# A two-layer hybrid decoder trunk: x taken in transposed, keys' blocks moved ahead of the values' blocks, one matmul per head for compressed values

## The chip, the cores and the metric

One Trainium2 chip, one core of it. The metric is the device time of one launch in microseconds, lower is better. Inputs and outputs lie in the chip's memory; arrays that the kernel prepares on the host before the launch (constants, and after the change a transposed copy of x) are not in the time.

## What is computed

x is 512 tokens by 1024 channels, float32. Two layers, each a token mixer and a feed-forward block, with RMS norms ahead of both:

```python
h = rms_norm(x, norm_mix_g[i]);  proj = h @ w_in[i]        # q_r k_r v_r g_r q_n kv_n gates
y_ret = (silu(g_r) * groupnorm(retention(rot(q_r), rot(k_r), v_r))) @ w_o_ret[i]
kc = gelu((blocks(k_c) + pos_k) @ w1_k) @ w2_k             # 31 blocks of 32 tokens, stride 16
vc = gelu((blocks(v_c) + pos_v) @ w1_v) @ w2_v
o_n = g0 * softmax(q kc + bias) vc + g1 * selected(q, k_s, v_s) + g2 * softmax(q k_w + bias) v_w
x = x + (sigmoid(m_a) * y_ret + sigmoid(m_b) * (o_n @ w_o_nsa[i])) @ w_out[i]
x = x + (silu(a) * b) @ w_ffn_out[i]                        # a, b from rms_norm(x) @ w_ffn_in[i]
```

NSA (the second mixer) has 16 heads of width 64 in two groups, with compressed keys and values of their own.

## The kernel before

Activations lie with channels on the partitions, x as 8 tiles of 128 channels by 512 tokens. A float32 product is made of three passes: each operand is split in a high part (a rounded copy, ScalarE) and the rest (VectorE), and `mm3` (L118 to L124) multiplies high by high, low by high and high by low. The norm's factor per token is not put into the activations: `make_h` splits x times the gain, and the factor 1/rms, kept as a row on all partitions in `rb`, is multiplied in where a product leaves PSUM. So a projection can start before the statistics are done, but what is read from its bank waits for `rb`.

A weight block comes as 1 MB into one of 3 raw buffers (`raw`, L91, on SP's queue) and is split by `cut` into pieces of 128x1024: the high part `wh` on ScalarE (L79), the low part `wl` on VectorE (L80). There are 3 buffers for pieces (`WH = 3`), so a fourth piece waits until TensorE has done with the first.

Start (`setup`, `start_x`): x is loaded as it lies, tokens on partitions, in 8 tiles; TensorE transposes it (L259, 32 transposes), ScalarE copies (L262) and splits it (L83), VectorE makes the low part (L84) and the sums of squares (L256). The gains and position embeddings are loaded as rows in 7 small DMAs and transposed as well (L158). GpSimd's queue writes the transposed x to memory (L266) for the residual.

`nsa_kv` is the stage that the change turns over, once per layer. On TensorE: `psc`, two products of 24 matmuls of 512 columns (compressed keys and values before compression); the statistics, `norm_stats` and `norm_bcast`, which makes `rb`; `psk`, two more (keys of the selected and the window branch); `compress` for keys and for values, 32 matmuls of 256 columns each (L377), whose inputs VectorE builds (`z` L352, `xa` L363, `p` or `pt` L80) and whose weight is four pieces (c0 to c3); `q0`, the first two query products of 24 each; then 96 matmuls of 304 columns for values and gates. `compress` and `q0` are generators and the calls of `next` in `nsa_kv` set their order in the code. A scheduler of the framework then sets each engine's final order from the dependences and its own estimates, so that pieces of neighbours may be interleaved.

After it the 16 heads run, with scores, softmax and products merged with gate projections that fill TensorE. Per head `nsa_finish` (L588) adds the compressed branch with two matmuls of 512 columns, one for the high part of the probabilities and one for the low part; `vc` holds a head's 31 rows at the partitions of its place in a quad and zeros elsewhere.

## Time and profile before

| | |
|---|---|
| median of 3 runs | 2456.5 us (2456.14 to 2457.05) |
| the profiled execution: its time, its span | 2455.72 us, 2453.9 us |
| TensorE busy, share of the span | 2404.7 us, 98% |
| VectorE, ScalarE, GpSimd busy | 57%, 42%, 10% |
| chain that ended last: TensorE, VectorE, ScalarE | 89%, 6%, 3% |
| layer 0: first matmul of the first product | at 17.28 us |
| layer 0: first matmul of values and gates | at 73.68 us |
| layer 1: first matmul of its first product | at 1231.50 us |
| layer 1: first matmul of values and gates | at 1285.61 us |

Matmuls overlap, so the recorded length of one (about 0.39 us for 512 columns) is longer than the time it takes from the next; the distance of two starts in a row tells that. Times in views are microseconds from the span's start. In the timeline's rows the columns are start, length (of all that the row merges), engine, line, operation, out<-in, shape, count, and in brackets the idle time ahead of it with what ended it.

### The profile page before, as it was taken

Reading aid. Unit: us, or ns where it says so; the run is one execution under the profiler, and the core shown is the slowest. Engines: PE = TensorE matmul, PEld = TensorE weight load, DVE = VectorE, ACT = ScalarE, POOL = GpSimd, SP = SyncE. Lnnn points to the kernel's source line nnn. Section 1 sums busy time; section 2 is a strip of 40 time slices with the busy share of each in tenths; the row PEclk is TensorE's granted clock in tenths of the full one; section 3 lists DMA queues with packets and bytes.
Section 4 is the critical chain, followed back from the end, with each engine's and each line's share of the span. In section 5 each row is a group of like instructions: output and inputs, shape, how many; then the busy total and the mean of one; then the engine's idle time right before and its main releaser. Section 6 shows DMA issues by size and latency. Waiting matters only on the chain.

```text
span 2453.9 us, 29372 instructions
## 1 busy us (share of the span) xinstructions
PE 2404.7 (98%) x11115; PEld 1956.1 (80%) x11115; DVE 1409.4 (57%) x2797; ACT 1025.3 (42%) x1862; POOL 252.2 (10%) x225
## 2 busy tenths in 40 slices
PE   7999999999999999999989999999999999999998
PEld 5877777888888878888878787778888877888887
DVE  6778886454574633333567878864545654434334
ACT  4666675233333432222346676642333333222222
POOL 1000000010020110110110000001100202101010
PEclk9999999999999999999999999999999999999999
DMA  7523224522342432323454322235223434223221
GB/s 230 149 74 87 74 69 102 165 85 96 98 142 95 155 102 87 103 87 99 128 141 120 94 79 73 74 102 156 90 93 106 159 110 139 86 86 103 86 95 60
DMA packets 234874, 262.47 MB, mean 107 GB/s; under 512 B 42276, under 2 KB 178637, under 8 KB 234733
## 3 DMA queue, kind: packets, MB, share of 16 engines
q1 hardware_dynamic: 220720, 236.93, 32.0%
q10 hardware_dynamic: 13244, 21.41, 2.4%
q8 instruction: 87, 1.43, 0.2%
q0 software_dynamic: 768, 2.27, 0.2%
q14 instruction: 55, 0.44, 0.1%
HBM read 235.36 MB, written 25.21 MB: 106 GB/s over the span
## 4 chain that ended last, share of the span: by engine, by line
PE 89%; DVE 6%; ACT 3%; issue 1%; POOL 1%; DMA 0%; SPq 0%; POOLq 0%; ACTq 0%; DVEq 0%
PE f L123 12%; PE f L122 12%; PE f L124 12%; PE a L124 8%; PE a L123 7%; PE a L122 7%; PE o L124 7%; PE o L122 7%; PE o L123 7%; PE t L573 2%; DVE p L553 1%; PE o L566 1%; PE o L565 1%; PE a L541 1%; PE a L542 1%
## 5 line engine op out<-in xcount | busy, mean ns | idle before, releaser
L79 ACT ACTIVATE wh<-wr 128x1024 fp32r<-128x1024 f32 (+3 forms) x406 | 397.2, 980 | 986.2 <-PE f L123 263.6
L80 DVE TENSOR_TENSOR wl<-wr,wh 128x1024 fp32r<-128x1024 f32 (+3 forms) x406 | 462.7, 1143 | 220.7 <-ACT wh L79 211.9
L122 PE MATMUL f<-hh,wh 128*128 128x512 f32 x936 | 373.4, 400 | 0.7 <-ACT wh L79 0.5
L124 PE MATMUL f<-hh,wl 128*128 128x512 f32 x936 | 371.5, 397 | 1.8 <-DVE wl L80 1.7
L123 PE MATMUL f<-hl,wh 128*128 128x512 f32 x936 | 370.7, 396 | 0.1
L124 PEld LDWEIGHTS f<-hh,wl 128*128 128x128 f32 x936 | 176.7, 189 | 44.0 <-DVE wl L80 4.1
L122 PEld LDWEIGHTS f<-hh,wh 128*128 128x128 f32 x936 | 176.9, 189 | 36.4 <-ACT wh L79 1.4
L123 PEld LDWEIGHTS f<-hl,wh 128*128 128x128 f32 x936 | 176.8, 189 | 33.9 <-DVE hl L84 0.6
L523 ACT ACTIVATE p<-p,nmx 128x512 f32<-128x512 f32 (+3 forms) x256 | 142.3, 556 | 67.1 <-DVE nmx L522 65.0
L80 DVE TENSOR_TENSOR pt<-t,pt 128x512 fp32r<-128x512 f32 (+3 forms) x256 | 123.5, 485 | 56.2 <-ACT pt L79 54.6
L124 PE MATMUL a<-hh,wl 128*128 128x512 f32 x360 | 144.7, 402 | 9.3 <-DVE wl L80 9.3
L122 PE MATMUL a<-hh,wh 128*128 128x512 f32 x360 | 144.8, 402 | 0.0
L123 PE MATMUL a<-hl,wh 128*128 128x512 f32 x360 | 144.5, 401 | 0.0
L79 ACT ACTIVATE pt<-t 128x512 fp32r<-128x512 f32 (+3 forms) x256 | 109.3, 429 | 71.8 <-PE t L573 66.9
L876 POOL TENSOR_TENSOR fa<-fa,rb 128x512 f32<-128x512 f32 x44 | 77.2, 1755 | 570.1 <-ACT fa L875 570.1
L522 DVE CUSTOM_DVE_ANT_0 p<-a,strip 128x512 f32<-128x512 f32 (+3 forms) x256 | 119.5, 484 | 18.1 <-PE a L542 11.5
L122 PE MATMUL o<-hh,wh 128*128 128x512 f32 x304 | 120.1, 395 | 0.0
L124 PE MATMUL o<-hh,wl 128*128 128x512 f32 x304 | 120.0, 395 | 0.0
L123 PE MATMUL o<-hl,wh 128*128 128x512 f32 x304 | 119.9, 395 | 0.0
L573 PE MATMUL t<-ident,p 128*128 128x128 f32 x640 | 113.7, 273 | 0.0
L573 PEld LDWEIGHTS t<-ident,p 128*128 128x128 f32 x640 | 81.3, 141 | 24.3 <-issue 2.2
L565 PE MATMUL o<-pt,vs 128*128 128x512 f32 (+3 forms) x256 | 91.4, 360 | 1.4 <-ACT pt L79 1.4
(423 smaller groups left out, 4859.4 us busy)
## 6 DMA issues: line engine op xcount, KB each, us to landing
wr<-in_w_in SPq DMA_DIRECT2D x66, 1024.0 KB, 5.3
wr<-in_w_ffn_in SPq DMA_DIRECT2D x44, 1024.0 KB, 5.2
wr<-in_w_ffn_out SPq DMA_DIRECT2D x18, 1024.0 KB, 5.0
wr<-in_w_o_ret SPq DMA_DIRECT2D x16, 1024.0 KB, 5.0
wr<-in_w_in SPq DMA_DIRECT2D x36, 256.0 KB, 4.0
strip<-bv SPq DMA_DIRECT2D x32, 256.0 KB, 5.1
gs<-mt ACTq DMA_DIRECT2D x32, 256.0 KB, 2.0
wr<-in_w_o_nsa SPq DMA_DIRECT2D x16, 512.0 KB, 7.3
```

Of the source, the lines that this page charges most:

```text
L79: self.nc.scalar.activation(hi, src, AF.Copy)
L80: (eng or self.nc.vector).tensor_sub(lo, src, hi.bitcast(F32))
L122: self.nc.tensor.matmul(ps, lh, rh, start=start and i == 0, stop=False)
L123: self.nc.tensor.matmul(ps, lh, rl, start=False, stop=False)
L124: self.nc.tensor.matmul(ps, ll, rh, start=False, stop=stop and i == n - 1)
L522: nc.vector.tensor_tensor_reduce(p, src, self.backwards(strip, w - 1, w), -1.0, BIG, ALU.add, ALU.min, nmx[:, c])
L523: nc.scalar.activation(p, p, AF.Exp, scale=-1.0, bias=nmx[:, c], accum_out=sm[:, c])
L541: nc.tensor.matmul(ps[:, :w], qh[:, ts], ks[:, br, :w], start=True, stop=False)
L542: nc.tensor.matmul(ps[:, :w], ql[:, ts], ks[:, br, :w], start=False, stop=True)
L565: nc.tensor.matmul(po[:, j * P :], lhs, th, start=br == 0 and j == 0, stop=False)
L573: nc.tensor.transpose(pt[:, (i - j) * P : (i - j + 1) * P], pr[br][i][:, j * P : (j + 1) * P], self.ident)
L876: nc.gpsimd.tensor_mul(t, t, self.rb)
```

## The change

Four things. (1) The host hands over x transposed (`c_xt`) and the gains and embeddings as columns (`c_cols`). The order on SP's queue becomes: the columns, two tiles of x, the first 1 MB block of weights, six tiles of x, the keys' block, the first queries' block, and then the compression weights. The 33 transposes, the copies, the small loads and the write of x to memory are gone. The sums of squares are now made as in the later norms: squares on ScalarE, seven additions on GpSimd (`acc_sq`), four matmuls with a column of ones. (2) In `nsa_kv`, in both layers, both pieces of the keys' block are cut at once and both products `psk` stand ahead of `compress`; the statistics' second half (`norm_bcast`) stands between them; `compress` of keys runs in one go behind the first query product, that of values behind the second. (3) `norm_bcast` transposes instead of multiplying by the identity. (4) High and low part of the compressed probabilities of two heads share a tile, rows 0 to 63 and 64 to 127, so `nsa_finish` needs one matmul; the splits in `nsa_cmp` become four operations on 64 partitions from two on 128, those in `compress` four pairs from eight.

```diff
@@ setup
-        rows = self.u("rows", w=P)
...
-        self.xnat = []
-        for hf in range(2):
-            for t in range(NT):
-                xt = self.u("xnat")
-                nc.sync.dma_start(xt, a["x"][0, t * P : (t + 1) * P, hf * 512 : (hf + 1) * 512])
-                self.xnat.append(xt)
-            if hf == 0:
-                load_rows()
-        self.setup_bias()
-        ps = self.tp()
-        nc.tensor.transpose(ps[:, :104], rows[:104, :], self.ident[:104, :104])
         self.cols = self.const("cols", [P, 104])
-        nc.vector.tensor_copy(self.cols, ps[:, :104])
+        nc.sync.dma_start(self.cols, a["c_cols"])
...
+        self.setup_bias()
@@ norm_bcast
         for t in range(NT):
-            nc.tensor.matmul(ps[:, t * P : (t + 1) * P], rep[:, t * P : (t + 1) * P], self.ident, start=True, stop=True)
+            nc.tensor.transpose(ps[:, t * P : (t + 1) * P], rep[:, t * P : (t + 1) * P], self.ident)
         nc.scalar.activation(self.rb, ps, AF.Copy)
@@ start_x
-        for k in range(KD):
-            if k % 4 == 0:
-                for t in range(NT):
-                    junk = self.u("junk")
-                    xn = self.xnat[k + t]
-                    nc.vector.tensor_tensor_reduce(junk, xn, xn, 1.0, 0.0, ALU.mult, ALU.add, ss[:, k + t : k + t + 1])
-            ps = self.mm() if k % 2 else self.tp()
-            for t in range(NT):
-                nc.tensor.transpose(ps[:, t * P : (t + 1) * P], self.xnat[4 * (k // 4) + t][:, (k % 4) * P : (k % 4 + 1) * P],
-                                    self.ident)
-            xt = self.u("xt")
-            nc.scalar.activation(xt, ps, AF.Copy)
-            h.append(self.make_h(xt, self.gmix[0][:, k : k + 1]))
-            if k == 2:
-                self.first_h = self.last_hi
-            nc.gpsimd.dma_start(self.xs[k], xt)
+        xts = [self.u("xt") for _ in range(KD)]
+        w = self.a["w_in"][0][:, C_KV : C_KV + 256].rearrange("(k p) n -> p k n", p=P)
+        for k in range(2):
+            last = nc.sync.dma_start(xts[k], self.a["c_xt"][k])
+        with self.tc.issue_after(last.ins):
+            raw = self.raw([(lambda v: v, w)], KD, 256)
+        with self.tc.issue_after(self.last_load.ins):
+            for k in range(2, KD):
+                self.last_x = nc.sync.dma_start(xts[k], self.a["c_xt"][k])
+        h = [self.make_h(xts[k], self.gmix[0][:, k : k + 1]) for k in range(2)]
+        with self.tc.issue_after(self.last_hi.ins):
+            self.first_w = [self.cut(raw[:, :, j * P : (j + 1) * P]) for j in range(2)]
+        h += [self.make_h(xts[k], self.gmix[0][:, k : k + 1]) for k in range(2, KD)]
+        self.first_h = self.last_hi
 
         def stats():
-            s2 = self.small("s2", NT)
-            nc.vector.tensor_add(s2, ss[:, :NT], ss[:, NT:])
-            self.norm_stats(ss=s2)
-            self.norm_bcast()
-
-        self.stats = stats
+            self.bias_rows()
+            acc = None
+            for xt in xts:
+                acc = self.acc_sq(acc, xt)
+            self.norm_stats(acc)
+
+        self.stats = stats, self.norm_bcast
@@ nsa_kv
-        self.stats()
+        self.stats[0]()
...
-        psk = [self.proj_t([self.cut(wk[:, :, :P])], 0, h, "a")]
+        with self.tc.issue_after(self.first_h.ins) if l == 0 else nullcontext():
+            wk = [self.cut(wk[:, :, br * P : (br + 1) * P]) for br in range(2)]
+        psk = [self.proj_t(wk, 0, h, "a")]
+        self.stats[1]()
+        psk.append(self.proj_t(wk, 1, h, "a"))
         comp = {kind: self.compress(l, kind, psc[i]) for i, kind in enumerate("kv")}
-        for kind in "kvk":
-            next(comp[kind])
-        psk.append(self.proj_t([self.cut(wk[:, :, P:])], 0, h, "a"))
+        fill = lambda n: [next(q0, None) for _ in range(n)]
+        next(comp["k"])
+        fill(9)
+        next(comp["k"])
+        next(comp["k"])
+        next(comp["v"])
         keys(0)
-        next(comp["k"])
-        for _ in range(2):
-            for _ in range(9):
-                next(q0, None)
-            next(comp["v"])
+        fill(9)
+        next(comp["v"])
+        next(comp["v"])
         keys(1)
@@ compress
-                    nc.scalar.activation(vc[r, q, :64], src, AF.Copy)
-                    nc.vector.tensor_sub(vc[r, q, 64:], src, vc[r, q, :64].bitcast(F32))
-                self.vc.append(vc)
+            for q in range(4):
+                r = slice(32 * q, 32 * q + 32)
+                nc.scalar.activation(vc[r, :, q % 2, :64], src[r], AF.Copy)
+                nc.vector.tensor_sub(vc[r, :, q % 2, 64:], src[r], vc[r, :, q % 2, :64].bitcast(F32))
+            self.vc = vc
@@ nsa_cmp
-        pc += [self.u("pch", F32R), self.u("pcl", F32R)]
-        self.split(pc[0], pc[1], pt2)
+
+        for r, o in ((slice(0, 64), slice(64, P)), (slice(64, P), slice(0, 64))):
+            x = self.u("pc", F32R)
+            self.split(x[r], x[o], pt2[r])
+            pc.append(x)
@@ nsa_finish
-        for i, x in enumerate(st["pc"]):
-            nc.tensor.matmul(po, self.vc[b][:, s], x, start=False, stop=i == 1)
+        nc.tensor.matmul(po, self.vc[:, b, s % 2], st["pc"][s // 2], start=False, stop=True)
@@ mix
-                nc.vector.tensor_add(xt, ps, self.ld("xo", self.xs[n]))
+                nc.vector.tensor_add(xt, ps, self.ld("xo", self.xs[n] if l else self.a["c_xt"][n]))
```

TensorE in layer 1, the kernel before, where the keys' second product (`a_10356`, pieces `wh_10352`, `wl_10353`) begins within compression of keys (`o_10325`, L377):

```order
L122 MATMUL a_10356<-hh_9912,wh_10352 128x512
L123 MATMUL a_10356<-hl_9913,wh_10352 128x512
L377 MATMUL o_10325<-wh_10391,p_10280 128x256
L124 MATMUL a_10356<-hh_9912,wl_10353 128x512
L122 MATMUL a_10356<-hh_9940,wh_10352 128x512
```

The keys' second product stands here in the middle of the keys' compression, and waits at its third row for `wl_10353`. The same place of the change: compression of keys (`o_10284`, now L362) at its third and fourth piece, behind it the second query product (`f_10393`):

```order
L362 MATMUL o_10284<-wl_10292,p_10219 128x256
L362 MATMUL o_10284<-wh_10313,p_10226 128x256
L362 MATMUL o_10284<-wl_10314,p_10226 128x256
...
L362 MATMUL o_10284<-wh_10317,p_10233 128x256
L362 MATMUL o_10284<-wl_10318,p_10233 128x256
...
L122 MATMUL f_10393<-hh_9829,wh_10389 128x512
L123 MATMUL f_10393<-hl_9830,wh_10389 128x512
L124 MATMUL f_10393<-hh_9829,wl_10390 128x512
```

The keys' products have moved ahead, all four pieces of a compression now follow each other, and the next product needs the fifth piece in a row.

VectorE in layer 0 of the change, from the low part of the last tile of x (`hl_154`) to the first use of `rb`; `wl_253`, `wl_257` are the keys' pieces, `wl_360` the queries', `wl_406` the first piece of compression, `var` and `rep` belong to the statistics:

```order
L84 SCALAR_TENSOR_TENSOR hl_154<-xt_106,cols,hh_153 128x512
L178 COPY near_212<-t_210 16x256
L179 COPY far_213<-t_210 16x384
L80 TENSOR_TENSOR wl_253<-wr_207,wh_252 128x1024
L80 TENSOR_TENSOR wl_257<-wr_207,wh_256 128x1024
L80 TENSOR_TENSOR wl_360<-wr_354,wh_359 128x1024
L80 TENSOR_TENSOR wl_406<-wr_403,wh_405 128x1024
L219 TENSOR_SCALAR var_246<-t_241 128x4
L269 TENSOR_SCALAR hrstd<-rstd 128x4
L225 COPY rep_285<-rstd 128x512
L337 TENSOR_TENSOR z_321<-f_157,rb 64x256 x4
```

Before, `var` stood ahead of three of the cuts of x and of every cut behind the keys' first piece; now it stands behind four cuts.

VectorE in layer 1 of the change, between the two compressions: the inputs of the values' compression (`pt`), the keys' split (`ks`), the second query product's end (`qd`), and the second to fourth piece of the values' compression (`wl_10440`, `wl_10462`, `wl_10466`):

```order
L80 TENSOR_TENSOR pt_10378<-xa_10374,pt_10378 128x4x64
L80 TENSOR_TENSOR ks_10132<-kd_10381,ks_10132 64x512
L80 TENSOR_TENSOR ks_10133<-kd_10381,kh_10382 64x512
L425 SCALAR_TENSOR_TENSOR qd_10418<-f_10393,rb 128x512
L80 TENSOR_TENSOR wl_10440<-wr_10433,wh_10439 128x1024
L80 TENSOR_TENSOR ql_10421<-qd_10418,qh_10420 64x512
L80 TENSOR_TENSOR wl_10462<-wr_10459,wh_10461 128x1024
L80 TENSOR_TENSOR ql_10427<-qd_10418,qh_10426 64x512
L80 TENSOR_TENSOR wl_10466<-wr_10459,wh_10465 128x1024
L80 TENSOR_TENSOR wl_10515<-wr_10511,wh_10514 128x912
```

Three of that compression's four pieces have moved behind the second query product's end, and the values' first piece (`wl_10515`) follows them at once.

## Rows read from the trace of the kernel before

**Rows 1.** The page: busy time (share of the span) and instructions of each engine, and the shares of the chain that ended last.

```profile
PE 2404.7 (98%) x11115; PEld 1956.1 (80%) x11115; DVE 1409.4 (57%) x2797; ACT 1025.3 (42%) x1862; POOL 252.2 (10%) x225
...
PE 89%; DVE 6%; ACT 3%; issue 1%; POOL 1%; DMA 0%; SPq 0%; POOLq 0%; ACTq 0%; DVEq 0%
```

**Rows 2.** The timeline of TensorE in layer 0, from the end of `psc` to the second keys' product.

```profile
35.09 0.39 PE L124 MATMUL f<-hh,wl 128*128 128x512 f32 x1
35.32 0.39 PE L124 MATMUL a<-hh,wl 128*128 128x512 f32 x1
...
44.04 0.28 PE L377 MATMUL o<-wh,p 128*128 128x256 f32 x1
49.17 0.79 PE L124 MATMUL a<-hh,wl 128*128 128x512 f32 x1 [4.86 <-DVE wl L80]
49.77 0.63 PE L122 MATMUL a<-hh,wh 128*128 128x512 f32 x1
...
53.18 0.63 PE L124 MATMUL a<-hh,wl 128*128 128x512 f32 x1
```

**Rows 3.** The windows view: stretch, its length, then busy time (instructions) of PE, PEld, DVE, ACT, POOL, the granted clock, the DMA engines' share, GB/s.

```profile
10.00:12.00 2.00, 0.93 (x4) 0.36 (x2) 0.00 (x0) 1.94 (x4) 0.00 (x0) 1.00 0.91 303
...
50.00:55.00 5.00, 5.00 (x15) 3.85 (x15) 4.23 (x5) 1.89 (x3) 0.00 (x0) 0.60 0.68 210
```

**Rows 4.** The timeline of layer 0's start, all engines: transposes, the first weight block, the low parts, the statistics' power.

```profile
6.61 0.47 PE L259 MATMUL o<-ident,xnat 128*128 128x128 f32 x1
...
16.17 1.06 ACT L79 ACTIVATE wh<-wr 128x1024 fp32r<-128x1024 f32 x1 [2.63 <-DMA wr<-in_w_in]
...
17.34 2.06 DVE L84 SCALAR_TENSOR_TENSOR hl<-xt,cols,hh 128x512 fp32r<-128x512 f32 x3
...
20.60 0.80 PE L124 MATMUL f<-hh,wl 128*128 128x512 f32 x1 [1.67 <-DVE wl L80]
...
26.95 1.48 POOL L235 TENSOR_TENSOR rstd<-var,mhalf 128x4 f32<-128x4 f32 x1 [4.18 <-DVE var L234]
```

**Rows 5.** The timeline of TensorE in layer 1: the wait for the statistics, the wait for the keys' second piece, values and gates.

```profile
1247.37 1.13 PE L244 MATMUL t<-ident,rep 128*128 128x128 f32 x8 [2.72 <-DVE hrstd L289]
...
1261.74 0.50 PE L124 MATMUL a<-hh,wl 128*128 128x512 f32 x1 [4.45 <-DVE wl L80]
...
1285.61 0.30 PE L122 MATMUL a<-wh,hh 128*128 128x304 f32 x1
...
1287.73 0.30 PE L124 MATMUL o<-wh,hl 128*128 128x304 f32 x1
```

**Rows 6.** The timeline of ScalarE in layer 0: `rb`.

```profile
36.88 0.60 ACT L245 ACTIVATE rb<-t 128x512 f32<-128x512 f32 x1 [0.53 <-PE t L244]
```

**Rows 7.** The timeline of VectorE in layer 0: the first piece of the values' block.

```profile
72.73 1.11 DVE L80 TENSOR_TENSOR wl<-wr,wh 128x912 fp32r<-128x912 f32 x1
```

**Rows 8.** The timeline of VectorE in layer 1, from the statistics to the first piece of the values' block.

```profile
1244.94 2.27 DVE L240 COPY rep<-rstd 128x512 f32<-128x512 f32 x1 [1.14 <-POOL rstd L235]
...
1249.16 1.75 DVE L352 TENSOR_TENSOR z<-f,rb 64x256 f32<-64x256 f32 x4 [0.75 <-ACT rb L245]
...
1256.84 2.37 DVE L363 TENSOR_TENSOR xa<-z,cols 128x124 f32<-128x124 f32 x8
1259.13 1.42 DVE L80 TENSOR_TENSOR pt<-xa,pt 128x256 fp32r<-128x256 f32 x4
...
1263.57 0.69 DVE L80 TENSOR_TENSOR ks<-kd,ks 64x512 fp32r<-64x512 f32 x1
...
1271.92 0.42 DVE L384 TENSOR_TENSOR gx<-o,gy 64x256 f32<-64x256 f32 x1
...
1276.32 0.69 DVE L441 SCALAR_TENSOR_TENSOR qd<-f,rb 128x512 f32<-128x512 f32 x1 [1.30 <-PE f L124]
1277.18 1.23 DVE L80 TENSOR_TENSOR wl<-wr,wh 128x1024 fp32r<-128x1024 f32 x1 [0.17 <-ACT wh L79]
1278.32 0.68 DVE L80 TENSOR_TENSOR ql<-qd,qh 64x512 fp32r<-64x512 f32 x1
...
1284.65 1.11 DVE L80 TENSOR_TENSOR wl<-wr,wh 128x912 fp32r<-128x912 f32 x1
```

**Rows 9.** One head's `nsa_finish` on TensorE, and the matmul behind it (timeline).

```profile
144.86 0.39 PE L588 MATMUL o<-pch,cv 128*128 128x512 f32 x1
145.09 0.39 PE L588 MATMUL o<-pcl,cv 128*128 128x512 f32 x1
145.32 0.39 PE L122 MATMUL f<-hh,wh 128*128 128x512 f32 x1
```

**Rows 10.** The low parts' matmuls of `nsa_finish` (groups by line and form: busy us, mean ns of one, idle before).

```profile
L588 PE MATMUL o<-pcl,cv 128*128 128x512 f32 x32 | 12.5, 391 | 0.0
```

**Rows 11.** The windows view, as in rows 3, of a stretch of the heads' stage.

```profile
200.00:300.00 100.00, 98.19 (x511) 79.93 (x511) 80.78 (x234) 66.32 (x163) 3.97 (x4) 1.00 0.25 72
```

**Rows 12.** The split of the compressed probabilities' low part (the view of that tile: count, shortest/median/longest ns, first and last start, shape).

```profile
L80 DVE TENSOR_TENSOR pcl<-t,pch x8: 683/692/693, 130.7 to 1566.5; 128x512 fp32r<-128x512 f32 x8
```

**Rows 13.** The timeline of GpSimd ahead of layer 1: two of the seven additions of squares.

```profile
1208.04 1.37 POOL L223 TENSOR_TENSOR sq<-sq,sq 128x512 f32<-128x512 f32 x1 [12.63 <-ACT sq L220]
...
1229.08 1.75 POOL L223 TENSOR_TENSOR sq<-sq,sq 128x512 f32<-128x512 f32 x1 [2.45 <-ACT sq L220]
```

**Rows 14.** The timeline of VectorE at the second of them.

```profile
1229.59 1.78 DVE L84 SCALAR_TENSOR_TENSOR hl<-strip,cols,hh 128x512 fp32r<-128x512 f32 x1
```

More of the change, by code (lines that the diff above doesn't have):

```diff
@@ L1 @@
 import math
-from contextlib import ExitStack
+from contextlib import ExitStack, nullcontext
 import numpy as np
@@ L164, in setup @@
                     "v": [self.cols[:, 72 + l * 16 : 88 + l * 16] for l in range(DEPTH)]}
+        self.ident = self.const("ident", [P, P])
+        nc.gpsimd.dma_start(self.ident, a["c_ident"])
+        self.setup_bias()
         self.mhalf = self.const("mhalf", [P, NT])
@@ L185, in setup_bias, with bias_rows @@
         tab = self.u("tab", w=HN)
-        nc.scalar.dma_start(tab[:32], a["rel_bias"])
+        nc.gpsimd.dma_start(tab[:32], a["rel_bias"])
         nc.vector.memset(tab[32:33], NEG)
         ohv = self.u("ohv", w=256)
-        nc.scalar.dma_start(ohv[:33], a["c_ohv"])
-        ps = self.mm()
+        nc.gpsimd.dma_start(ohv[:33], a["c_ohv"])
+        self.bias_in = tab, ohv
+    def bias_rows(self):
+        nc = self.nc
+        tab, ohv = self.bias_in
+        ps = self.tp()
         nc.tensor.matmul(ps[:HN, :256], tab[:33], ohv[:33], start=True, stop=True)
@@ L234, in norm_stats @@
         nc.vector.tensor_scalar(var, ss, 1.0 / D, 1e-6, ALU.mult, ALU.add)
-        self.last_rstd = nc.gpsimd.tensor_tensor(self.rstd, var, self.mhalf, ALU.pow)
+        nc.gpsimd.tensor_tensor(self.rstd, var, self.mhalf, ALU.pow)
     def norm_bcast(self):
@@ L280, in nsa_kv @@
         view = lambda c, n, k0=0, kt=KD: w[k0 * P : (k0 + kt) * P, c : c + n].rearrange("(k p) n -> p k n", p=P)
-        if l == 0:
-            with self.tc.issue_after(self.first_h.ins):
-                wc = self.wcols(w, 0, KD, C_KV, 256)
-        else:
-            wc = self.wcols(w, 0, KD, C_KV, 256)
+        wc = self.first_w if l == 0 else self.wcols(w, 0, KD, C_KV, 256)
         psc = [self.proj_t(wc, j, h, "f") for j in range(2)]
-        wk = self.raw([(lambda v: v[:, :, :P], view(C_KV + 256, P)), (lambda v: v[:, :, P:], view(C_KV + 512, P))], KD, 256)
-        self.stats()
+        with self.tc.issue_after(self.last_x.ins) if l == 0 else nullcontext():
+            wk = self.raw([(lambda v: v[:, :, :P], view(C_KV + 256, P)), (lambda v: v[:, :, P:], view(C_KV + 512, P))], KD, 256)
+        self.stats[0]()
         nc.vector.tensor_scalar(self.hrstd, self.rstd, 0.5, None, ALU.mult)
@@ L414, in compress @@
                                      start=c == 0, stop=c == 1)
-            for g in range(2):
-                vc = self.tile("cv", 2, F32R).rearrange("p (s d) -> p s d", s=4)
-                nc.gpsimd.memset(vc.bitcast(F32), 0.0)
-                for q in range(4):
-                    r = slice(32 * q, 32 * q + 32)
-                    src = po[r, g * 64 : g * 64 + 64]
-                    nc.scalar.activation(vc[r, q, :64], src, AF.Copy)
-                    nc.vector.tensor_sub(vc[r, q, 64:], src, vc[r, q, :64].bitcast(F32))
-                self.vc.append(vc)
+            vc = self.tile("cv", 2, F32R).rearrange("p (g e d) -> p g e d", g=2, e=2)
+            nc.gpsimd.memset(vc.bitcast(F32), 0.0)
+            src = po[:, :P].rearrange("p (g d) -> p g d", g=2)
+            for q in range(4):
[3 more added lines that the diff above has]
+            self.vc = vc
     def nsa_q(self, l, h, quad, qs):
@@ L854, in stats @@
             self.norm_stats(acc)
-            self.norm_bcast()
-        self.stats = stats
+        self.stats = stats, self.norm_bcast
         return x, hn
@@ L871, in hidden @@
                 if k0 == 0 and c == 0 and j == 0:
-                    self.stats()
+                    for part in self.stats:
+                        part()
                 t = self.u("fa")
@@ L900, in stats @@
             self.norm_stats(acc)
-            self.norm_bcast()
-        self.stats = stats
+        self.stats = stats, self.norm_bcast
         return hn
@@ L1015, in constants, with layouts @@
     }
+def layouts(inputs):
+    rows = [inputs["norm_mix_g"].reshape(-1, P), inputs["norm_ffn_g"].reshape(-1, P), inputs["norm_final_g"].reshape(-1, P),
+            inputs["cmp_pos_k"].reshape(-1, P), inputs["cmp_pos_v"].reshape(-1, P)]
+    return {"c_xt": np.ascontiguousarray(inputs["x"][0].T).reshape(KD, P, T),
+            "c_cols": np.ascontiguousarray(np.concatenate([rows[0][:8], rows[0][8:], *rows[1:]]).T)}
 def build_program(tc, args, out):
@@ L1034 @@
     arrays.update(constants())
+    arrays.update(layouts(inputs))
     args = {}
```

16 lines of the change are left out of this document (2 added, 14 removed).

## The prediction

> **What bounds the kernel now.** I read the page first: TensorE is busy 98% of the span and carries 89% of the chain that ended last, VectorE 6% [rows 1]. So two things shorten this kernel: matmuls that vanish where TensorE has no gap, and gaps that close. The timelines of `nsa_kv`, read next, show the gaps. In layer 0 TensorE starts its first product at 17.28 us but its third matmul only at 20.60, behind the low part of the weight [rows 4]. It waits 4.86 us for the keys' second piece, then runs eleven matmuls 0.43 apart (49.17, 49.77 ... 53.18) where 35.09 and 35.32 stand 0.23 apart [rows 2]. The windows view gives a mean granted clock of 0.60 from 50 to 55 [rows 3]: the half level (1.2 GHz) behind the gap, then the full one (2.4). Layer 1 has waits of 2.72 for the statistics and of 4.45 for that piece [rows 5]. Last I read who ends each gap: VectorE. From `rb` on it runs almost without a pause through the inputs of both compressions, the keys' splits and the cuts, and its cut at 1284.65 releases the values at 1285.61 [rows 8, 5]. So inside `nsa_kv` I compare VectorE's chain with TensorE's products.
>
> The profiled run took 2455.72 us, 0.8 under the median. Terms are differences, made against it. 0.2%, some 4.9 us, is what a measurement of this kernel can tell from no change.
>
> **The start (part 1).** Transposes (the fourth at 6.61 belongs to the old path) and copies leave; the stream of DMAs decides. It moves 0.303 MB per us [rows 3]. Four tiles, 1.05 MB, take 3.5 us and have landed before 6.61 [rows 4], so it starts about 3.1. Ahead of the end of the first weight block now stand columns 0.05, two tiles 0.52, the block 1.05 and GpSimd's small loads 0.15 MB: 1.77/0.303 = 5.8 us, landing at 9.0. `wh` takes 1.06 and `wl` 1.23 [rows 4, 8]: the third matmul starts at about 11.3, **9.3 earlier** than 20.60. The six tiles left, 1.57 MB, land by 14.2 and their splits follow at about 0.69 each [rows 4]. With some matmuls at half speed the first product ends near 18.5, the next two near 24.1 and 29.7 (24 matmuls by 0.233 are 5.6).
>
> Does `rb` come earlier as well? The keys' block lands near 15.8, the squares run on ScalarE behind its first `wh`, eight by about 0.6 (`rb` on as many elements [rows 6]), and the seven additions on GpSimd take 1.37 to 1.75 each [rows 13]: from about 18 to 28 or 30. The diff doesn't show, but the order does, that `var` stands on VectorE behind `wl_406`, the first compression piece, and that needs a buffer which only the keys' first product gives back, at 29.7. So `wl_406` and a little more end at 32.1, the power takes 1.48 [rows 4], `rep` 2.27 [rows 8], the four transposes 0.45, `rb` 0.60 [rows 6]: it ends at **about 37.2**, where it ended at 37.48 before. The early start is not passed on to VectorE's chain.
>
> **nsa_kv's order (part 2), layer 0.** VectorE, from `rb` to the values' first cut: for each compression `z` 1.75, `xa` 2.37, `p` or `pt` 1.42; the gelu about 1.5 (four short operations, `gx` is 0.42); `kd` and twice `ks` 2.0; two queries' ends `qd` and four `ql`, 0.62 each with overlap, 3.7; and eight pieces, 1.14 from start to start (1277.18 to 1278.32), 9.1 [rows 8]. Together **27.4**. Before, the stretch took 72.73 - 37.48 = 35.2 [rows 6, 7]; with nine pieces that is 28.5 of work and 6.7 of pauses. Walking both engines through the new order I keep 4.4 of them: the second to fourth piece of a compression alternate with TensorE (its 8 matmuls give a buffer back), and both query ends wait for their product. The cut starts at 37.2 + 27.4 + 4.4 = 69.0 instead of 72.73: **-3.7**. The wait of 4.86 is gone, but what ended at its end, VectorE's chain, stays.
>
> TensorE now idles instead around the values' compression (about 3.6 and 2.6 us), since its second to fourth piece stand behind the second query's end on VectorE. A gap of 4.86 was followed by the half level [rows 2]; I put the same here, and the values start in it. Sixteen to eighteen of their matmuls, 0.14 each at the full level (1285.61 to 1287.73 is 15 steps [rows 5]) and by the ratio 0.43 to 0.23 about 0.26 at half, lose 0.12: +2.2. The half level that followed the old gap (11 by 0.2) lay under VectorE's chain. Layer 0: -3.7 + 2.2 = **-1.5**.
>
> **Layer 1.** No start to win. The statistics' transposes now stand behind the keys' first product, and `rb` ends 1.6 later than its old 1249.1 (the `z` behind it began at 1249.16 [rows 8]), at 1250.75. Two pieces, 2.3, now stand between `rep` and `z` and outlast transposes and `rb` by about 1.4, so the pauses are 4.4 + 1.4: the cut comes at 1250.75 + 27.4 + 5.8 = 1284.0, was 1284.65: -0.7. Half level in the values: +2.2. Layer 1: **+1.5**. Ends for the chain's term: no pause gives -6.5, layer 0's old 6.7 on top of the 1.4 gives +1.6.
>
> **norm_bcast (part 3).** The products by the identity are recorded as eight for 1.13 us [rows 5], the transposes should be half of that, some 0.45 less. Two of four places stand behind `rb`'s chain and are counted above; the two in the feed-forward: **-0.9**, between 0 (VectorE late anyway) and -1.3.
>
> **nsa_finish (part 4).** 16 heads in two layers lose one matmul of 512 columns each, 32 in all [rows 10]. Not its 0.39 counts but its distance, 144.86 to 145.09 to 145.32: 0.23 [rows 9]. The heads' stage has TensorE 98% busy at the full clock, VectorE 81% [rows 11], so nothing else ends it: 32 by 0.23 = **-7.4**, half of it if every second one hid a wait. The split of probabilities becomes two pairs on 64 partitions: one more 0.69 [rows 12] on VectorE per quad and as much on ScalarE, eight quads. It is hidden by VectorE's 19% of idle time; uncovered it costs 5.5. Fewer splits for the values' compression lie beside the values' products: nothing.
>
> **The sum**: -1.5 + 1.5 - 0.9 - 7.4 = -8.3, so 2447.4 for the profiled run and **2448 us** for the median.
>
> One price has two readings, the additions of squares on GpSimd. Rows show one at 1.37 and one at 1.75, with VectorE's `hl` at 1.78 beside the latter, against 0.69 alone [rows 13, 14, 4]. My walk takes them as slowed but overlapping, done by 30. If each held VectorE off entirely, seven of them plus four two-input cuts would follow one another from 18: 9.6 + 4.9 = 14.5, to 32.5, and `var`, `rb` and the cut come up to 4.4 later. The Trainium skill, SBUF — State Buffer, section "Who interferes with whom", speaks for that reading: a VectorE instruction with two inputs in SBUF and a GpSimd instruction that reads SBUF share one read interface, and the one that issues second is fully blocked. By it the sum would be -3.9; the 1.78 beside the 1.75 agrees in direction, and I keep it as a rival.
>
> **The rivals.**
> A, the sum: 2448, its own range 2443 to 2452 (pauses a few us either way). Chance 0.52.
> B, VectorE's pauses go, and values start at the full clock: layer 0 -8.1 (37.2 + 27.4 = 64.6), layer 1 -6.5, parts 3 and 4 -8.3, that is -22.9, so 2433. For it: all pieces but the keys' are loaded early, and four pieces now follow each other. Against: three buffers of pieces, seven of eight need one back. All of it or half (2440): 0.20.
> C, the additions block VectorE as above, in layer 0: +4.4, 2452.4; or, beside it, VectorE keeps its old 6.7 of pauses (+2.3 a layer), 2457: no change that shows, the saved matmuls are spent in `nsa_kv`. For it: pauses before came from the same buffers. 0.20.
> D, slower: TensorE's short gaps recur through the values' stage, since each of their pieces waits on the same engine that is late with queries, and the clock stays at half for all 96 matmuls of both layers: 96 by 0.12, less the 2.2 counted, 9.3 a layer, +18.6 on the sum: 2466. It decides if cuts of 912 come over 4 us apart. Before, values ran at the full distance from 1285.61 on [rows 5]; so 0.08.
>
> **How the numbers follow.** The forecast is A. B's middle and C lie within 2432 to 2457; left out are D, the last of B and of C, under 2 in 10. Faster by over 0.2% (under 2451.6): most of A, B, a little of C: 0.70. Same: the rest of A, most of C: 0.22. Slower: D: 0.08.
>
> **What would show it.** Right: third matmul near 11.3; `rb` ending within 1 us of 37.2 although TensorE started 9 earlier; the first 128x912 cut near 69 and 1284; TensorE waiting in the values' compression on VectorE's `pt` or `wl`; a granted clock below 1 in the windows that follow; one row per head in `nsa_finish` and 98% busy around it. Wrong: `rb` well before 35 (then `var` did not stand behind the piece), the cut before 66 or 1281 (B), `rb` past 40 (C), heads' stage not shorter by 7, or values 0.26 apart to their end (D).

## The result

The changed kernel takes **2427.3 us** (median of 4 runs, 2425.45 to 2429.37), the kernel before 2456.3: a ratio of 0.9882, 95% interval 0.9865 to 0.9899, 29 us faster. The forecast was 2448 with a range of 2432 to 2457. The direction was right, the size was not: the gain is 3.5 times the 8.3 us of the sum, and the time lies 5 us under the range. The profiled run took 2427.7 us. Times of whole kernels below are medians of runs at a granted clock of 0.99 or more; one run, of the changed kernel with 128 unused bytes, took 3919.4 us at 0.556 and is left out. The profiled run's page, the lines that answer to rows 1:

```profile
PE 2371.8 (98%) x11042; PEld 1938.4 (80%) x11042; DVE 1410.7 (58%) x2779; ACT 1029.9 (42%) x1862; POOL 258.8 (11%) x224
...
PE 89%; DVE 6%; ACT 3%; issue 1%; POOL 1%; DMA 0%; SPq 0%; POOLq 0%; ACTq 0%; DVEq 0%
```

TensorE has lost 73 instructions and 32.9 us of busy time; the shares have not moved, so neither view tells where the time went.

Layer 0 first, since most of the prediction's working is there. TensorE in the changed kernel (timeline, columns as in the rows of before):

```profile
11.96 0.79 PE L124 MATMUL f<-hh,wl 128*128 128x512 f32 x1
...
36.12 0.66 PE L229 MATMUL t<-ident,rep 128*128 128x128 f32 x4 [1.80 <-DVE rep L225]
...
60.36 0.39 PE L362 MATMUL o<-wh,pt 128*128 128x256 f32 x1 [3.10 <-DVE pt L80]
...
64.66 0.58 PE L362 MATMUL o<-wl,pt 128*128 128x256 f32 x1 [2.53 <-DVE wl L80]
...
68.07 0.30 PE L122 MATMUL a<-wh,hh 128*128 128x304 f32 x1
```

The third matmul starts at 11.96, 8.6 earlier than 20.60 [rows 4]. The gap of 4.86 at the keys' second piece [rows 2] is gone, and two gaps, 3.10 and 2.53, stand in the values' compression. The values start at 68.07, at 73.68 before. ScalarE's `rb` in the same kernel:

```profile
36.82 0.60 ACT L230 ACTIVATE rb<-t 128x512 f32<-128x512 f32 x1 [5.53 <-PE t L229]
```

It ends at 37.42 and ended at 37.48 before [rows 6]: TensorE is 8.6 us ahead, and `rb` comes at the same time. The additions of squares on GpSimd and VectorE around them show why:

```profile
18.71 11.36 POOL L208 TENSOR_TENSOR sq<-sq,sq 128x512 f32<-128x512 f32 x7
32.70 1.04 POOL L220 TENSOR_TENSOR rstd<-var,mhalf 128x4 f32<-128x4 f32 x1 [2.63 <-DVE var L219]
```

```profile
21.70 2.23 DVE L80 TENSOR_TENSOR wl<-wr,wh 128x1024 fp32r<-128x1024 f32 x1 [2.77 <-ACT wh L79]
25.83 1.71 DVE L80 TENSOR_TENSOR wl<-wr,wh 128x1024 fp32r<-128x1024 f32 x1 [1.90 <-ACT wh L79]
31.32 1.23 DVE L80 TENSOR_TENSOR wl<-wr,wh 128x1024 fp32r<-128x1024 f32 x1 [3.79 <-ACT wh L79]
32.47 0.15 DVE L219 TENSOR_SCALAR var<-t 128x4 f32<-128x4 f32 x1
33.85 2.21 DVE L225 COPY rep<-rstd 128x512 f32<-128x512 f32 x1
...
67.08 2.63 DVE L80 TENSOR_TENSOR wl<-wr,wh 128x1024 fp32r<-128x1024 f32 x3
```

Seven additions run from 18.71 to 30.07. Two cuts beside them are recorded with 2.23 and 1.71, alone with 1.23. The third and the fourth addition by themselves:

```profile
21.55 1.29 POOL L208 TENSOR_TENSOR sq<-sq,sq 128x512 f32<-128x512 f32 x1
```

```profile
22.93 2.16 POOL L208 TENSOR_TENSOR sq<-sq,sq 128x512 f32<-128x512 f32 x1
```

The first cut is recorded from 21.70 and ends at 23.93, 1.09 behind the end of the third addition (22.84). The fourth addition ends at 25.09, 1.16 behind that cut. So they took turns and did not run side by side. `var` does stand behind a cut (31.32), but the sums ended so late that this cost little. The last row merges three cuts, the second of which, at 68.22, is the values' first piece.

Two more places. The granted clock around the values' start (windows view; columns as in rows 3) falls to the half level after the gaps, but is back before the bulk of the values' matmuls:

```profile
60.00:65.00 5.00, 2.11 (x10) 1.82 (x11) 4.91 (x9) 4.40 (x7) 0.00 (x0) 0.60 0.00 0
65.00:70.00 5.00, 5.00 (x29) 4.76 (x29) 4.65 (x6) 4.39 (x7) 0.00 (x0) 0.72 0.56 141
70.00:85.00 15.00, 15.00 (x110) 14.68 (x109) 10.63 (x25) 9.17 (x22) 0.53 (x1) 1.00 0.64 206
```

And a stretch that the change does not touch, 250 us of layer 0's feed-forward, where TensorE has no gap and the clock is full. Before, then after:

```profile
900.00:1150.00 250.00, 250.00 (x1078) 202.67 (x1077) 94.58 (x104) 63.42 (x74) 25.68 (x15) 1.00 0.29 93
```

```profile
900.00:1150.00 250.00, 250.00 (x1094) 205.13 (x1093) 97.14 (x107) 64.77 (x76) 27.20 (x15) 1.00 0.29 96
```

The same 512-column matmuls, 1094 instead of 1078 in the same time. From start to start they average 232.4 ns before (228 to 241) and 228.9 after (225 to 232). Nobody waits in either. This is where the prediction had no term at all.

Cut at six points of the program (starts, from the timelines: in each layer the last 304-column matmul of the values and the last matmul of `nsa_finish`; between the layers the last `fa` that GpSimd makes in layer 0; and the end of ScalarE's last `p`, 3.5 us ahead of the span's end in both), the 28.1 us between the two profiled programs split like this:

| stretch | before, us | after, us | difference |
|---|---|---|---|
| layer 0 up to the values' end | 89.96 | 84.31 | -5.7 |
| layer 0, heads | 333.56 | 330.41 | -3.2 |
| layer 0, retention and feed-forward | 770.57 | 761.51 | -9.1 |
| layer 1 up to the values' end | 107.78 | 105.51 | -2.3 |
| layer 1, heads | 333.48 | 330.38 | -3.1 |
| layer 1, the rest | 815.14 | 810.26 | -4.9 |

Fourteen of the 28 us lie in the third and the last stretch, where the change touches little beside one `norm_bcast` each.

### The profile page after: what moved, and what is told of

The parts are those of the page before. It is cut to its first block, busy times and chain, and to the rows that moved or that the text cites. A ratio compares the mean times of both kernels' runs of the same rounds, so it can differ in the third digit from the quotient of the medians.

```text
span 2425.8 us, 29172 instructions
## 1 busy us (share of the span) xinstructions
PE 2371.8 (98%) x11042; PEld 1938.4 (80%) x11042; DVE 1410.7 (58%) x2779; ACT 1029.9 (42%) x1862; POOL 258.8 (11%) x224
## 4 chain that ended last, share of the span: by engine, by line
PE 89%; DVE 6%; ACT 3%; issue 1%; POOL 1%; DMA 0%; SPq 0%; POOLq 0%; ACTq 0%; DVEq 0%
PE f L122 11%; PE f L123 11%; PE f L124 11%; PE o L123 8%; PE a L123 8%; PE o L122 8%; PE a L122 8%; PE o L124 8%; PE a L124 7%; PE t L560 2%; DVE p L540 1%; PE o L553 1%; PE o L552 1%; DVE wl L80 1%; PE a L528 1%
## 5 line engine op out<-in xcount | busy, mean ns | idle before, releaser
L122 PE MATMUL f<-hh,wh 128*128 128x512 f32 x936 | 373.9, 399 | 3.0 <-ACT wh L79 2.9
L124 PE MATMUL f<-hh,wl 128*128 128x512 f32 x936 | 369.3, 395 | 1.2 <-DVE wl L80 1.1
L124 PEld LDWEIGHTS f<-hh,wl 128*128 128x128 f32 x936 | 176.9, 189 | 41.5 <-DVE wl L80 3.6
L122 PEld LDWEIGHTS f<-hh,wh 128*128 128x128 f32 x936 | 177.0, 189 | 38.2 <-ACT wh L79 4.7
L123 PE MATMUL a<-hl,wh 128*128 128x512 f32 x336 | 132.5, 394 | 0.0
L122 PE MATMUL a<-hh,wh 128*128 128x512 f32 x336 | 132.2, 394 | 0.0
L124 PE MATMUL a<-hh,wl 128*128 128x512 f32 x336 | 131.2, 390 | 0.0
L123 PE MATMUL o<-hl,wh 128*128 128x512 f32 x328 | 129.3, 394 | 0.0
L122 PE MATMUL o<-hh,wh 128*128 128x512 f32 x328 | 128.9, 393 | 0.0
L124 PE MATMUL o<-hh,wl 128*128 128x512 f32 x328 | 128.0, 390 | 0.0
```

Of the source, the lines that this page charges most:

```text
L122: self.nc.tensor.matmul(ps, lh, rh, start=start and i == 0, stop=False)
L123: self.nc.tensor.matmul(ps, lh, rl, start=False, stop=False)
L124: self.nc.tensor.matmul(ps, ll, rh, start=False, stop=stop and i == n - 1)
```

## The experiments

What could shorten matmuls that nobody touched? The built programs' memory maps differ in one thing that reaches every product. No view of a trace shows addresses; these are from the maps, and the sizes can be followed in the kernel's text. The old start used a small tile `s2` in six buffers of 32 bytes per partition. The change drops it, and the pool of weight buffers (`wr`, `wh`, `wl`), which lies behind, starts at 178784 instead of 178976. The activations' pool starts at 21920 in both. All tiles in these pools are multiples of 256 bytes apart, so one number describes a program: weights minus activations modulo 256, 128 before and 192 after.

**The place alone, on either kernel.**

```diff
-        self.cols = self.const("cols", [P, 104])
+        self.cols = self.const("cols", [P, 104]); nc.vector.memset(self.small("pad", 16, bufs=1), 0.0)
```

16 elements are 64 bytes; other sizes stand with each run.

> The kernel before with one unused tile of 64 bytes per partition added to the pool of small tiles, so that the buffers of weights behind it lie 64 bytes higher, at 96 beyond a multiple of 128 as in the changed kernel, not at 32; no instruction but one short memset is added. Theory P (place): the distance of the 512-column matmuls depends on where the weight pieces lie; it falls from 232.4 ns to about 229 in the long products, some 4,800 matmuls by about 3 ns, so 2442 us. Rival H (history): the distance depends on how engines fall into step after the gaps, and the place does nothing: 2456, with 232.4 ns.

Measured: 2436.7 us against 2455.9, ratio 0.9922 (0.9907 to 0.9937): **19 us from one unused tile**, without any of the change, and 5 under the 2442 of theory P.

> The changed kernel with an unused tile of 192 bytes, which puts the buffers of weights back exactly where they lay in the kernel before. Theory P: the distance goes back to about 232.4 ns, 2441 us, and what is left to the change itself is 15 of its 29 us. Rival H: 2427, distances of 228.9 as in the changed kernel.

Measured: 2444.6, ratio to before 0.9953 (0.9936 to 0.9969), 17 us slower than the changed kernel. The windows, of the kernel before with 64 bytes and of the changed kernel with 192:

```profile
900.00:1150.00 250.00, 250.00 (x1094) 205.14 (x1093) 96.92 (x107) 64.40 (x76) 27.00 (x15) 1.00 0.29 94
```

```profile
900.00:1150.00 250.00, 250.00 (x1078) 202.70 (x1077) 95.30 (x105) 63.40 (x74) 25.25 (x14) 1.00 0.29 95
```

1094 and 1078 have changed sides with the place. Rival H falls for this stretch: the order of work and its gaps do not set the distance here. At the old place the change itself is worth 2455.9 - 2444.6 = 11.3 us.

**Own place, or place against the activations?** One kernel moves both pools (the pad goes to the first pool), another moves both and sets their difference to 0.

> The kernel before with the 64 unused bytes in the first pool, so that activations and weights both move up by 64 (weights to 96 beyond a multiple of 128, activations from 32 to 96). Theory P (the weights' own place decides): 228.9 ns in the long products and 2437 as with the weights alone moved. Rival R (their place relative to the activations decides): 232.4 ns and 2456.

Measured: 2457.1, ratio 1.0003 (0.9993 to 1.0012), 232.4 ns. The weights lie where they were fast in the run before, and nothing is gained: my theory P fell, and R stands.

> The changed kernel with the weights' buffers 64 bytes higher, at 32 beyond a multiple of 128 as in the kernel before, but at another multiple of 256. If places repeat every 128 bytes: 232.4 ns, 2444. If they repeat every 256 or not at all: another distance, anything from 2427 to 2444.

Measured: 2403.8, ratio 0.9782 (0.9767 to 0.9796). None of my numbers; the difference is 0 modulo 256 here, and this is the best place of all.

```profile
900.00:1150.00 250.00, 250.00 (x1105) 207.10 (x1104) 97.21 (x107) 64.86 (x76) 27.02 (x15) 1.00 0.29 96
```

> The changed kernel with the weights' buffers 32 bytes higher, at a multiple of 128. If 64-byte rows are what counts (32 and 96 both lie in the middle of one), a place at their start should be at least as good as 96: 228.9 ns or less, 2427 or down to 2415 if all products take the shortest distance seen, 226. Rival: only the one place of the changed kernel is good, then 2444.

Measured: 2447.0, ratio 0.9957 (0.9942 to 0.9972), 233.3 ns. The first reading, 2427 or less, fell: a multiple of 128 as an address is no merit. The rival's 2444 was near.

> The kernel before with 128 unused bytes ahead of the weights' buffers, so that weights and activations differ by a multiple of 256 bytes, as in the changed kernel with 64 (2403.8). Theory R (only the difference modulo 256 counts, whatever the program): 226.7 ns in the long products; the same 41 us as between the changed kernel at the old place (2444.6) and that one, so 2415. Rival: the 2403.8 belonged to that program alone, and here the gain is at most the 19 us of 64 bytes: 2437 or more.

Measured: 2413.2, ratio 0.9825 (0.9810 to 0.9839), 226.7 ns. R foretold it to 2 us, on the other program.

> The changed kernel with weights and activations both moved, so that they still differ by a multiple of 256 bytes but lie at 224 beyond a multiple of 256, not at 160. Theory R: 2404, 226.7 ns. Rival P (the place itself counts): any other time, up to 2447.

Measured: 2403.3, ratio 0.9785 (0.9770 to 0.9799), 226.7 ns. With the difference kept at 0, the place itself does nothing. The difference of the kernel before with 128 bytes is 256 more than that of the changed kernel with 64, and both have 226.7; the kernel before with 64 bytes and the changed kernel also lie 256 apart, and both have 228.9. That is what carries the "modulo 256".

**The other four differences**, the changed kernel with 96, 128, 160 and 224 bytes.

> The changed kernel with 96 unused bytes: weights and activations differ by 32 modulo 256. Theory M (multiples of 64 are good, odd multiples of 32 bad): bad like 224, 233 ns and 2445 to 2447. Rival N (nearness to 0 counts): close to 0's 226.7, under 2415.

> The changed kernel with 128 unused bytes: difference 64. Theory M: a multiple of 64, like 192, 229 ns and 2427; 128 with its 232.4 stays unexplained. Rival N: between 0 and 128, 229 to 230 ns, about 2425. Rival: periodic in 128 as seen from 64, then like 192, 228.9, the same number for another reason.

> The changed kernel with 160 unused bytes: difference 96. Theory M: 233 ns, 2445 to 2447. Rival N: between 64 and 128, 230 to 232 ns, 2430 to 2440.

> The changed kernel with 224 unused bytes: difference 160. Theory M: 233 ns, 2445 to 2447. Rival N: between 128 (232.4) and 192 (228.9), about 231 ns, 2436.

All eight differences of the changed kernel together (distance: mean from start to start of the 512-column matmuls of L122 to L124, from 900 to 1150 us, which is layer 0):

| weights minus activations, modulo 256 | us | distance, ns | least to most |
|---|---|---|---|
| 0 | 2403.8 | 226.7 | 225 to 228 |
| 32 | 2448.7 | 233.3 | 231 to 235 |
| 64 | 2443.2 (one run) | 233.3 | 233 to 234 |
| 96 | 2451.8 | 234.3 | 230 to 238 |
| 128 (as before) | 2444.6 | 232.4 | 228 to 241 |
| 160 | 2450.6 | 233.3 | 230 to 238 |
| 192 (as after) | 2427.3 | 228.9 | 225 to 232 |
| 224 | 2447.0 | 233.3 | 230 to 236 |

Neither theory holds whole. Odd multiples of 32 are all slow (M), but of the multiples of 64 only 0 and 192 are fast. N falls at 32, and the period of 128 falls at 64 (233.3, not 228.9).

The table is one stretch of layer 0, and it does not speak for the whole program at every difference. In the feed-forward of layer 1, TensorE without a gap and at the full clock, before, after, and the changed kernel with 64 bytes:

```profile
2180.00:2300.00 120.00, 120.00 (x518) 97.32 (x517) 46.91 (x53) 30.67 (x37) 14.44 (x8) 1.00 0.30 97
```

```profile
2180.00:2300.00 120.00, 120.00 (x516) 97.01 (x516) 47.05 (x53) 31.97 (x38) 14.41 (x8) 1.00 0.27 89
```

```profile
2180.00:2300.00 120.00, 120.00 (x531) 99.46 (x530) 46.40 (x53) 30.82 (x36) 12.61 (x7) 1.00 0.27 88
```

From start to start these average 232.4, 233.3 and 226.7 ns: the changed kernel, at 228.9 in layer 0, is here no faster than the one before. The two other kernels with the difference 192 show the same 228.9 in layer 0 and 233.3 in layer 1, so this belongs to the place and the stage, not to the order or the gaps. (The kernels at 128 differ among themselves there, 232.4 or 233.3.) At 0 both layers have 226.7, in all five kernels. What else sets the distance at 192 stays open. It fits the table of stretches, where the last stretch gains 4.9 us and the third 9.1.

**The parts, at the old place.** Part 4 alone on the kernel before (`vc`, the splits and `nsa_finish` as in the change's diff):

> The kernel before with part 4 alone: one matmul per head for the compressed values, and the new splits. The weights' buffers lie as before. The term as predicted, 32 matmuls by 0.23: -7.4, 2449. Rival: the heads' stage gives back only what the changed kernel showed there, 2.7 and 2.5 us in its two layers, since VectorE's and ScalarE's extra split per quad comes into the path: 2451.

Measured: 2452.3, ratio 0.9985 (0.9976 to 0.9994): -3.6 us. In its trace the heads' stage is 2.5 and 2.3 us shorter (points as in the table above), 4.8 together. The new group of matmuls in the changed kernel, which answers to rows 10:

```profile
L574 PE MATMUL o<-pc,cv 128*128 128x512 f32 x32 | 12.6, 393 | 0.0
```

32 are left of 64, but the term of 7.4 was not reached. Whether the new splits ate the rest was the next question, put by issuing the merged matmul twice, so that the compressed branch counts double:

```diff
-        nc.tensor.matmul(po, self.vc[:, b, s % 2], st["pc"][s // 2], start=False, stop=True)
+        nc.tensor.matmul(po, self.vc[:, b, s % 2], st["pc"][s // 2], start=False, stop=False)
+        nc.tensor.matmul(po, self.vc[:, b, s % 2], st["pc"][s // 2], start=False, stop=True)
```

> The changed kernel with 64 unused bytes, where each head issues its merged matmul for the compressed values twice (so the compressed branch counts double): a second one put back, with the new splits kept. Theory: one such matmul per head costs its whole distance, 32 by 0.23 = 7.4, so 2411, and what part 4 lacked of 7.4 was paid by its splits. Rival: such a matmul costs only the 3.6 to 5 us that part 4 alone gave back, 2407 to 2409, since something else sets part of the heads' stage.

Measured: 2407.3 against 2403.8, +3.5, near the rival. The heads' stage grows by 2.5 us in each layer, 5.1 together. The splits are cleared: with them kept, the matmul costs in that stage what part 4 gave back there (4.8), 0.16 us and not 0.23. The medians alone would say half, 0.11, but they hold differences of other stages too. In these two traces the values of layer 0 end at 83.00 and 84.93, which the edit does not touch.

The rest is waits. Between the two kernels the matmuls of L574 and L575 differ by 3.7 us in layer 0, while the time from other matmuls of the heads to their next grows by 1.2 where the matmul is missing, spread over several groups, among them those that wait for the softmax (`o<-pt,vs`) and the gate products. TensorE shows as 98% busy there [rows 11], but some of a removed matmul's time goes into waits; that they come from the chain through VectorE and ScalarE is argued, not shown.

The order, taken out of the changed kernel and put alone into the one before:

```diff
-        self.stats[0]()
+        self.stats[0](); self.stats[1]()
...
-        psk = [self.proj_t(wk, 0, h, "a")]
-        self.stats[1]()
-        psk.append(self.proj_t(wk, 1, h, "a"))
...
+        psk = [self.proj_t([self.cut(wk[:, :, :P])], 0, h, "a")]
+        comp = {kind: self.compress(l, kind, psc[i]) for i, kind in enumerate("kv")}
+        for kind in "kvk":
+            next(comp[kind])
+        psk.append(self.proj_t([self.cut(wk[:, :, P:])], 0, h, "a"))
...
```

> The changed kernel with the order of nsa_kv put back (keys' second product within the compression, both halves of the statistics where they stood). Start, transposes and merged matmul stay. Theory: the order is worth what layer 1 showed, where no start is won, 2.4 us, so 2.4 to 5 in both layers: 2430 to 2432. Rival R1: the early start reaches the end only through the new order, then layer 0 loses its 5.6 and layer 1 its 2.4: 2435. Rival R2: the order is worth nothing and the start carried all of layer 0's 5.6: 2427 to 2429.

Measured: 2433.8, 6.6 us slower than the changed kernel at the same place, so near R1. Against the kernel before at that place (2436.7) start, transposes and merged matmul together bring 2.8, and the merged matmul alone brought 3.6: the start with the transposes brings nothing that these medians can tell.

> The kernel before with part 2 alone, the new order in both layers; weights lie as before. Theory: the order alone is worth what the changed kernel lost without it less what needs the early start: layer 1's 2.4 in each layer, 2451. Rival: the order is worth its full 6.6 without the start: 2449. Rival: it needs the start, and alone makes layer 0 later, since the statistics' second half comes behind a product: 2456 or more.

Measured: 2455.6, ratio 1.0000 (0.9990 to 1.0010): the order alone brings nothing either. `rb` in the two kernels, first the order alone, then the start without the order:

```profile
41.21 0.60 ACT L245 ACTIVATE rb<-t 128x512 f32<-128x512 f32 x1
```

```profile
41.62 0.60 ACT L230 ACTIVATE rb<-t 128x512 f32<-128x512 f32 x1 [6.41 <-PE t L229]
```

Each half of the change by itself makes `rb` of layer 0 over 4 us later than the 36.88 of before [rows 6], and the values start at 75.48 and 75.74, later than 73.68. Up to the end of layer 0's values the order alone costs 2.4 us, and the start without the order 3.7 against the kernel before at its place. Only together do they keep `rb` at 36.82, with the keys' second product almost done (its last matmul starts at 38.92); why each alone makes `rb` later no run separates. By medians 11.3 - 3.6 = 7.7 us are a joint gain of parts 1 to 3; by the stretches of the kernel with 192 bytes it is 6.4. Either is good to a few us. Where no start is won, in layer 1, the order alone gives 1.1.

**Is it `rb` that holds layer 0?** Squares added on VectorE, first piece of compression behind `rep`, at difference 0:

```diff
-                acc = self.acc_sq(acc, xt)
+                sq = self.u("sq")
+                nc.scalar.activation(sq, xt, AF.Square)
+                if acc is None:
+                    acc = sq
+                else:
+                    nc.vector.tensor_add(acc, acc, sq)
...
-        nc.vector.tensor_copy(rep.rearrange("p (t c) -> p t c", c=P),
+        self.hold = nc.vector.tensor_copy(rep.rearrange("p (t c) -> p t c", c=P),
...
+                    with self.tc.issue_after(self.hold.ins):
+                        hv, lv = self.cut(rv[:, :4])
```

> The changed kernel with 64 unused bytes, where layer 0's squares are added on VectorE and not on GpSimd, and the first piece of compression is cut behind the copy of 1/rms. Theory: layer 0's chain hangs on rb; rb ends at about 32 where it ended at 38, and values start 4 to 6 us earlier: 2399 against 2404. Rival: TensorE's products are the limit by then, rb earlier gives under 1 us: 2403 or more.

Measured: 2400.9, ratio 0.9775 (0.9760 to 0.9789), 2.9 under the same kernel with the sums on GpSimd (2403.8): the fastest version here, 55 us under the kernel before. `rb` and the first of the values, first with the sums on GpSimd, then with the sums on VectorE:

```profile
37.45 0.60 ACT L230 ACTIVATE rb<-t 128x512 f32<-128x512 f32 x1 [5.52 <-PE t L229]
```

```profile
68.80 0.30 PE L122 MATMUL a<-wh,hh 128*128 128x304 f32 x1
```

```profile
31.17 0.58 ACT L230 ACTIVATE rb<-t 128x512 f32<-128x512 f32 x1
```

```profile
57.14 0.58 PE L376 MATMUL o<-wh,pt 128*128 128x256 f32 x1 [3.15 <-DVE pt L80]
...
61.44 0.58 PE L376 MATMUL o<-wl,pt 128*128 128x256 f32 x1 [2.01 <-DVE wl L80]
...
65.04 0.46 PE L122 MATMUL a<-wh,hh 128*128 128x304 f32 x1
```

`rb` comes 6 us earlier, the values 4, and the whole is 2.9 shorter. About half passes through. These are single traces: in ten kernels that differ up to there in the place of buffers alone, `rb` of layer 0 ends between 35.2 and 39.0 and the values between 83.0 and 86.0; here they end at 31.8 and 81.8. The rival's end is nearly as close as the theory's: the two gaps in the values' compression stay, so more than `rb` holds the values. That it is VectorE's chain behind `rb` is what the gaps say (they end with `pt` and `wl`).

## Why the prediction missed, step by step

**The step that failed** is the one that the sum rested on without saying so: that a matmul of 512 columns keeps its distance of 0.23 us wherever the change does not act. In the feed-forward of layer 0 it fell from 232.4 to 228.9 ns. It was rounded to two digits in the rows, and 3.5 ns of 232 went unseen. The sum had no term for the place of buffers, and the map of the program would have shown that dropping `s2` moves every weight buffer by 192 bytes. Undoing that alone costs 17 us, making it alone gains 19. No rival held it either; B's 2433 had the size of a gain like this for a reason that isn't it.

**At the old place the time is near the forecast, in part by luck.** 2444.6 stands against the forecast 2448 with its own range of 2443 to 2452, but two errors went against each other. The traces of both (before, and the changed kernel with 192 bytes) allow the terms to be compared:

- *The start*: right. Third matmul forecast at 11.3, measured 11.96; "not passed on": `rb` forecast to end at 37.2, measured 37.42. The reason given, `var` behind `wl_406`, was the smaller one: the sums ended at 30.07, TensorE's products with ones ran from 31.18 to 32.13, and the cut delayed `var` by about 0.4 more.
- *The additions*: forecast done by 30, measured 30.07, but not by the reading that was forecast. They were taken as slowed and overlapping; the rows above show turns, which is rival C's reading. One after the other, seven additions at 1.37 and the two cuts at 1.2 that fall in the stretch are 12.0 us; measured were 11.36. By the Trainium skill's rule (SBUF — State Buffer, "Who interferes with whom") a VectorE instruction with two inputs in SBUF and a GpSimd instruction that reads SBUF block each other; the trace agrees. What kept C's 32.5 away is that two cuts, not four, came due then. C's price of 4.4 does not follow from its 32.5 either, since the forecast has `wl_406` end at 32.1 anyhow.
- *`nsa_kv`, layer 0*: -1.5 forecast, -4.6 measured (values' end 89.96 and 85.40). VectorE's first cut of the values was forecast at 69.0. It starts at 68.34 at the old place (68.22 after), so the chain was sized well: -4.4 against -3.7. The half-clock term of +2.2 was too large. The half level came, but most of it fell on the 256-column matmuls of the compression. At the old place it lasts to about 70:

```profile
65.00:70.00 5.00, 5.00 (x24) 5.00 (x25) 4.77 (x6) 3.86 (x6) 0.00 (x0) 0.50 0.52 138
```

  The values' stage takes 17.02 us there, 16.28 before: +0.7. (In the changed kernel it takes 16.24.)
- *Layer 1*: +1.5 forecast, -0.8 measured. The half-clock term is 0.7 again (17.01 against 16.27), and the rest is a chain with fewer pauses.
- *`nsa_finish`*: -7.4 forecast, -3.6 measured alone by medians, and in the two heads' stages -4.8 alone and -4.6 here, nearer the end that the text gave as "half of it if every second one hid a wait". I took the upper end because of 98% busy; the put-back matmul shows that about a third hides.
- *`norm_bcast`*: transposes fell from 1.13 for eight records [rows 5] to 0.66 and 0.60 for four, as forecast; retention, feed-forward and the rest are 1.0 us shorter in both layers together, forecast -0.9. That size is not shown: the same stretches differ from before by +0.4 and -1.3 together in two kernels without this part.

So the missing 20.7 us are 17 of place and 3.4 of terms that nearly cancelled: 5.4 too little gain forecast in `nsa_kv` (2.9 of it the half-clock term), 2.8 too much in the heads, 0.1 elsewhere, and 0.7 between traces and medians.

Rival D was out: the distance in the values' stage is 0.14 from 70 on.

## To carry to other kernels

Where TensorE is 98% busy, measure the distance of its matmuls to the nanosecond, over a long gapless stretch of each layer, before and after any edit; 1.5% there was worth more here than the whole reordering. An edit that adds or drops a tile moves the pools behind it: compare the memory maps, and hold the difference between stationary and moving operands when parts of a change are to be priced. Price a removed instruction by putting one back, not by its length: in the heads' stage here, at 98% busy, about a third of it was hidden.

## What the runs showed of the hardware

- The distance of 512-column float32 matmuls (of the rounded kind) in layer 0's feed-forward depended on the address of the weight tile minus that of the activation tile modulo 256 bytes: 226.7 ns at 0, 228.9 at 192, 232.4 to 234.3 at the other six multiples of 32. Absolute places did not matter in the two runs that moved both pools. Why 192 differs from 64, and which accesses meet, no run here shows.
- At 0 both layers' feed-forward kept one distance (226.7, in all five kernels). At 192 it was 228.9 in layer 0 and 233.3 in part of layer 1, in all three kernels with that difference, so the difference alone does not fix it.
- The distance is no single number but a short repeating pattern (225 to 232 at 192, 228 to 241 at 128), nearly the same in every kernel with the same difference, and at 0 it goes on over gapless rows of over 1500 matmuls.
- A VectorE subtraction with both inputs in SBUF and GpSimd's additions took turns: a cut of 1.2 us was recorded with 2.23, and the addition behind it took 2.16 instead of 1.29.
- Two parts of a change that each gained nothing clear of noise alone (2455.6 against 2455.9; 2.8 where the merged matmul alone gave 3.6) gained 6 to 8 us together.
